# Loading one block of A in two lots, into idle result buffers, in the opening of a tuned matmul

## The chip, the cores and the metric

One core of one Trainium2 chip. The metric is device time in microseconds (us) of one execution; medians are over several runs. A profile is of one execution; its "span", from first to last instruction, is 1.7 us shorter than the device time of the same execution.

A load is issued by GpSimd; DMA engines then move the data, and the load has landed when the last of its 16 completions has counted up its semaphore (a counter that others can wait for). In the lines shown, PE is TensorE, PEld its weight loads, DVE VectorE, ACT ScalarE, POOL GpSimd; a timeline has start, length, engine, line, what, and in brackets the idle time before it and what ended that.

## The reference

```python
def setup_inputs():
    m, k, n = 4096, 4096, 4096
    # a (m, k), b (k, n), bias (n,), all float32, normally distributed
def reference(a, b, bias):
    return np.tanh(np.matmul(a, b) + bias)
```

The kernel casts A and B to 16-bit floats while loading. The product is 8192 TensorE matmuls of 128 x 128 by 128 x 512.

## The kernel before

Only the opening matters. There TensorE must start before A and B are there, so it works on eight row tiles (group 0: tiles 0 to 3, group 1: tiles 4 to 7) and takes the 32 depth tiles of A and B in blocks. All these loads but those of B's first two depth tiles go through one queue, GpSimd's. A load of A is four issues, one for each quarter of the partitions; VectorE then transposes it, and only then can TensorE use it.

```python
    AN = 3                                   # buffers "an" for loads of A
    anat = ctx.enter_context(tc.tile_pool(name="anat", bufs=AN))
    opool = ctx.enter_context(tc.tile_pool(name="opool", bufs=4))   # results "o_sb"
    ...
    def load_a(m0, nmb, t0, nt):
        an = anat.tile([P, nmb, nt * QP], fp16, name="an")
        for t, n in split(t0, nt):
            for q in (0, 2, 1, 3):
                ...
                nc.gpsimd.dma_start(out=an[ds(q * QP, QP), :, ...], in_=...)
        return an
    ...
    def pump():                              # issue loads in order while a buffer is free
        while queue and (queue[0][0] is None or live[0] < AN):
            ...
    # the order of the loads
    want_a("g1a", 2, 4 * P, 2 * Q, 0, BL)    # group 1, depth tiles 0-3, two row tiles
    want_a("g1a2", 2, 6 * P, 2 * Q, 0, BL)
    want_a("g1b", G, 4 * P, G * Q, BL, BL)   # group 1, depth tiles 4-7
    for i in range(BL):
        want(load_b_next)                    # B, depth tiles 4-7
    want_a("g0b", G, 0, G * Q, BL, BL)       # group 0, depth tiles 4-7   <- the change
    want_a("g0c", G, 0, G * Q, KS, KM - KS)  # group 0, depth tiles 8-15
    for u in range(KS, KM, 2):
        want(lambda u=u: load_b_all(u, 2))   # B, depth tiles 8 and 9 first
    ...
```

The four result buffers hold something else first: the first block of group 0 ("nat"), which TensorE transposes at 6.5 to 9.8 us. Then they lie idle until the main loop.

Of the kernel before, what the change touches and what calls it, by code (L numbers as in the profile page):

```python
# [14 lines left out]
P = 128  # L15
Q = 4
QP = 32
NB = 512
fp32 = mybir.dt.float32
fp16 = mybir.dt.float16  # L20
# [3 lines left out]
def kernel(  # L24
# [18 lines left out]
    G = 4  # L43
    KS = 8
    AN = 3
    BL = 4
# [5 lines left out]
    anat = ctx.enter_context(tc.tile_pool(name="anat", bufs=AN))  # L52
    atp = ctx.enter_context(tc.tile_pool(name="atp", bufs=4))
    biasp = ctx.enter_context(tc.tile_pool(name="biasp", bufs=2))
    opool = ctx.enter_context(tc.tile_pool(name="opool", bufs=4))
# [22 lines left out]
    def split(t0, nt):  # L78

        low = [(t, BL) for t in range(t0, min(t0 + nt, KS), BL)]  # L80
        t = max(t0, KS)
        return low + ([(t, t0 + nt - t)] if t0 + nt > t else [])

    def load_a(m0, nmb, t0, nt):
        an = anat.tile([P, nmb, nt * QP], fp16, name="an")
        for t, n in split(t0, nt):
            for q in (0, 2, 1, 3):
                k = t * P + q * BL * QP if t < KS else P * KS + (q * (KT - KS) + t - KS) * QP
                src = a[ds(m0, nmb * QP), ds(k, n * QP)]
                nc.gpsimd.dma_start(  # L90
                    out=an[ds(q * QP, QP), :, ds((t - t0) * QP, n * QP)],
                    in_=src.rearrange("(mb p) k -> p mb k", p=QP),
                )
        return an

    def transpose_a(at, an, mb0, t0, nt):

        for t, n in split(t0, nt):
            order = "P mb (k t) -> P mb t k" if t < KS else "P mb (t k) -> P mb t k"
            nc.vector.transpose(  # L100
                at[:, ds(t, n), :].rearrange("P t (mb p) -> P mb t p", p=QP),
                an[:, ds(mb0, Q), ds((t - t0) * QP, n * QP)].rearrange(order, k=QP),
            )
# [9 lines left out]
    queue, live, staged = [], [0], {}  # L113

    def pump():
        while queue and (queue[0][0] is None or live[0] < AN):
            key, uses, load = queue.pop(0)
            made = load()
            if key is not None:
                live[0] += 1  # L120
                staged[key] = [made, uses]

    def want_a(key, uses, *where):
        queue.append((key, uses, lambda: load_a(*where)))

    def want(load):
        queue.append((None, 0, load))

    def turn(at, key, mb0, t0, nt):
        pump()  # L130
        transpose_a(at, staged[key][0], mb0, t0, nt)
        staged[key][1] -= 1
        if not staged[key][1]:
            live[0] -= 1
            pump()

    def mm(ps, at, bt, t, j, start, stop):
# [4 lines left out]
    def finish(ps, addend, mi, c0, w=NB, o_sb=None, queues=(nc.sync,)):  # L142
# [22 lines left out]
    ats = [  # L165
        bpool.tile([P, KT, P], fp16, name=f"atx_{m}", tag=f"b_{4 + m}") for m in range(G)
    ] + [atp.tile([P, KT, P], fp16, name="at") for m in range(G)]
# [41 lines left out]
    def down(ps, ms, t0, t1, done):  # L209
        for m in ms:  # L210
            for j in range(J):
                for t in range(t0, t1):
                    mm(ps[m][j], ats[m], b_cur, t, j, False, t == t1 - 1)
                done(ps[m][j], m, j)
# [73 lines left out]


    want_a("g1a", 2, 4 * P, 2 * Q, 0, BL)  # L290
    want_a("g1a2", 2, 6 * P, 2 * Q, 0, BL)
    want_a("g1b", G, 4 * P, G * Q, BL, BL)
    for i in range(BL):
        want(load_b_next)
    want_a("g0b", G, 0, G * Q, BL, BL)
    want_a("g0c", G, 0, G * Q, KS, KM - KS)
    for u in range(KS, KM, 2):
        want(lambda u=u: load_b_all(u, 2))
# [3 lines left out]
    for t in (KM, KM + 8):  # L302
        want_a(("g1", t), G, 4 * P, G * Q, t, 8)
        want(lambda t=t: load_b_all(t, TB))
        if t > KM:
            want(lambda: load_bias(bias_bc, 0, nc.gpsimd))
        want(lambda t=t: load_b_all(t + TB, TB))
    for m in g0:
        want_a(("g0", m), 1, m * P, Q, KM, KT - KM)
    todo = [(c, mi) for c in range(NC) for mi in range(MT) if (c, mi) >= (0, 2 * G)]  # L310
    pump()


    for i in range(G):
        turn(ats[G + i], "g1a2" if i > 1 else "g1a", i % 2 * Q, 0, BL)
    down(ps, g0, BL - 1, BL, put_aside)
    for i in range(G):
        turn(ats[G + i], "g1b", i * Q, BL, BL)
# [1 line left out]
    one_by_one(ps, g1, 0, BL, 0)  # L320
    across(ps, g1, BL, KS - 1, 0)
    for m in g0:
        turn(ats[m], "g0b", m * Q, BL, BL)
    down(ps, g1, KS - 1, KS, put_aside)


# [127 lines left out]
```

## Time and profile before

| | before |
|---|---|
| device time, median (six runs) | 1781.6 us (1781.4 to 1782.1) |
| span of the profiled execution | 1780.6 us |
| TensorE busy | 1774.4 us, 100% |
| GpSimd busy (writing loads) | 872.5 us, 49% |
| VectorE busy | 763.7 us, 43% |

A busy TensorE can hide short stalls, since each matmul is recorded with 0.38 us while the next one starts 0.215 us behind it. So the reading goes by the distance between starts. The prediction below shows the lines. Its "chain of waits" is the work that ended last, followed back from the last instruction, each piece to what released it.

### The profile page before, as it was taken

To read this page: it belongs to the slowest core of one execution; us is meant where nothing else is said; L and a number is where in the kernel's file an instruction comes from. 1 tells how busy PE (TensorE), PEld (TensorE's weight loads), DVE (VectorE), ACT (ScalarE), POOL (GpSimd) and SP (SyncE) were. 2 spreads that over 40 slices of the span, in tenths; PEclk is the share of its full clock that TensorE was granted. 3 is DMA by queue.
4 is the path that set the end of the run, shared out by engine and by line. 5 is a ranking of instruction groups with operands and counts; after the bars stand their busy time and mean duration, and the time that the engine had idled before them with its cause. 6 is when DMAs were issued, how large, how long until landed. Compare 5 with 4: busy or idle time off the path is not lost.

```text
span 1780.6 us, 20859 instructions
## 1 busy us (share of the span) xinstructions
PE 1774.4 (100%) x8254; PEld 807.0 (45%) x8254; DVE 763.7 (43%) x682; ACT 172.9 (10%) x281; POOL 872.5 (49%) x1618
## 2 busy tenths in 40 slices
PE   9999999999999999999999999999999999999999
PEld 4444444444444444444444444444444444444444
DVE  3574443444334443444344443444344443444342
ACT  2021000000000000000000000000000000000001
POOL 7465566544565554444456554444544445444510
PEclk9999999999999999999999999999999999999999
DMA  9999999976999877767699997766777667766731
GB/s 183 205 193 177 173 162 166 141 125 110 166 176 164 145 112 116 118 116 120 113 168 173 159 149 116 119 115 109 129 116 121 107 108 121 119 114 109 117 77 42
DMA packets 281393, 238.94 MB, mean 134 GB/s; under 512 B 159056, under 2 KB 231760, under 8 KB 281296
## 3 DMA queue, kind: packets, MB, share of 16 engines
q0 software_dynamic: 243280, 167.88, 69.9%
q1 hardware_dynamic: 37728, 69.62, 11.0%
q8 instruction: 64, 1.05, 0.3%
q14 instruction: 33, 0.27, 0.0%
q10 hardware_dynamic: 288, 0.13, 0.0%
HBM read 337.64 MB, written 67.11 MB: 227 GB/s over the span
## 4 chain that ended last, share of the span: by engine, by line
PE 98%; DMA 1%; POOL 0%; issue 0%; DVE 0%; ACT 0%; POOLq 0%; DVEq 0%
PE ps L415 93%; PE ps L138 5%; DMA an<-in_a_dram 1%; DMA b<-in_b_dram 0%; POOL an L90 0%; POOL nat L246 0%; ACT o_sb L152 0%; DVE atx L100 0%; DVE o_sb L149 0%; POOL b L69 0%; POOL ident L264 0%; POOLq L264 0%; DVEq L149 0%; DVEq L100 0%; POOLq L438 0%
## 5 line engine op out<-in xcount | busy, mean ns | idle before, releaser
L415 PE MATMUL ps<-b,at 128*128 128x512 f16 x7712 | 1657.8, 378 | 0.0
L90 POOL DMA_DIRECT2D an<-in_a_dram x1492 | 805.9, 547 | 797.1 <-DVE at L100 558.6
L415 PEld LDWEIGHTS <-at 128*128 128x128 f16 x7712 | 754.6, 98 | 903.3
L100 DVE STREAM_TRANSPOSE at<-an 128x512 f16<-128x512 f16 (+1 forms) x380 | 565.5, 1539 | 78.2 <-DMA an<-in_a_dram 78.2
L149 DVE TENSOR_TENSOR o_sb<-ps,bias_bc 128x512 f32<-128x512 f32 (+1 forms) x243 | 165.6, 683 | 907.3 <-PE ps L415 697.7
L152 ACT ACTIVATE o_sb<-o_sb 128x512 f32<-128x512 f32 (+1 forms) x243 | 151.4, 624 | 1501.2 <-DVE o_sb L149 1501.2
L73 POOL DMA_DIRECT2D b<-in_b_dram x104 | 56.2, 544 | 14.1 <-DMA an<-in_a_dram 7.0
L138 PE MATMUL ps<-b,atx 128*128 128x512 f16 x256 | 56.2, 379 | 0.6 <-DVE atx L100 0.6
L138 PE MATMUL ps<-b,at 128*128 128x512 f16 x256 | 55.6, 379 | 0.0
L138 PEld LDWEIGHTS <-at 128*128 128x128 f16 x256 | 25.0, 98 | 30.2
L138 PEld LDWEIGHTS <-atx 128*128 128x128 f16 x256 | 24.8, 98 | 30.6 <-DVE atx L100 1.6
L100 DVE STREAM_TRANSPOSE atx<-an 128x512 f16<-128x512 f16 (+2 forms) x12 | 16.3, 1399 | 11.7 <-DMA an<-in_a_dram 11.7
L69 POOL DMA_DIRECT2D b<-in_b_dram x12 | 7.8, 654 | 22.4 <-PE ps L415 22.3
L152 ACT ACTIVATE spill<-spill 128x512 f32<-128x512 f32 x16 | 9.9, 630 | 84.4 <-DVE spill L149 84.4
L149 DVE TENSOR_TENSOR spill<-ps,spill 128x512 f32<-128x512 f32 x16 | 10.2, 674 | 6.2 <-PE ps L138 6.2
L181 DVE TENSOR_TENSOR spill<-spill,bias_bc 128x512 f32<-128x512 f32 x16 | 10.3, 681 | 3.5 <-DMA bias_bc<-in_bias_dram 3.5
L173 ACT COPY spill<-ps 128x512 f32<-128x512 f32 x16 | 8.0, 624 | 12.8 <-PE ps L138 12.8
L228 PE MATMUL ps<-zeros 128*128 128x512 f16 (+1 forms) x14 | 4.7, 504 | 1.3 <-DVE zeros L221 1.3
L176 DVE TENSOR_TENSOR spill<-ps,spill 128x512 f32<-128x512 f32 x8 | 4.8, 674 | 0.0
L228 PEld LDWEIGHTS <-zeros 128*128 128x128 f16 x14 | 1.6, 130 | 3.7 <-issue 2.5
L246 POOL DMA_DIRECT2D nat<-in_a_dram x4 | 2.3, 587 | 0.8 <-POOLq L438 0.8
L239 DVE CAST b<-spill 128x1024 f16<-128x1024 f32 x1 | 0.7, 694 | 4.3 <-DMA spill<-in_b_dram 4.3
(14 smaller groups left out, 9.1 us busy)
## 6 DMA issues: line engine op xcount, KB each, us to landing
an<-in_a_dram POOLq DMA_DIRECT2D x480, 192.0 KB, 5.1
out_dram<-o_sb SPq DMA_DIRECT2D x239, 256.0 KB, 2.7
an<-in_a_dram POOLq DMA_DIRECT2D x960, 32.0 KB, 2.7
b<-in_b_dram POOLq DMA_DIRECT2D x94, 256.0 KB, 8.1
b<-in_b_dram POOLq DMA_DIRECT2D x6, 1024.0 KB, 12.5
an<-in_a_dram POOLq DMA_DIRECT2D x32, 128.0 KB, 5.3
out_dram<-spill SPq DMA_DIRECT2D x16, 256.0 KB, 5.1
an<-in_a_dram POOLq DMA_DIRECT2D x12, 256.0 KB, 8.3
```

The source lines that it names most:

```text
L69: queue.dma_start(out=dst, in_=src[:, ds(t0 % BL, nt), :])
L73: nc.gpsimd.dma_start(out=bt[t0 // TB][ds(q * QP, QP), ds(t0 % TB, nt), :], in_=src.rearrange("(t p) n -> p t n", p=QP),)
L90: nc.gpsimd.dma_start(out=an[ds(q * QP, QP), :, ds((t - t0) * QP, n * QP)], in_=src.rearrange("(mb p) k -> p mb k", p=QP),)
L100: nc.vector.transpose(at[:, ds(t, n), :].rearrange("P t (mb p) -> P mb t p", p=QP), an[:, ds(mb0, Q), ds((t - t0) * QP, n * QP)].rearrange ...
L138: nc.tensor.matmul(ps, at[:, t, :], bt[t // TB][:, t % TB, ts(j, NB)], start=start, stop=stop)
L149: nc.vector.tensor_tensor(out=o_sb[:, piece], in0=ps[:, piece], in1=addend[:, piece], op=mybir.AluOpType.add)
L152: nc.scalar.activation(o_sb[:, piece], o_sb[:, piece], mybir.ActivationFunctionType.Tanh)
L173: nc.scalar.copy(aside(m, j), ps)
L176: nc.vector.tensor_tensor(out=aside(m, j), in0=ps, in1=aside(m, j), op=mybir.AluOpType.add)
L181: nc.vector.tensor_tensor(out=aside(m, j), in0=aside(m, j), in1=bias_bc[:, ts(j, NB)], op=mybir.AluOpType.add)
L228: nc.tensor.matmul(ps[:, ds(0, w)], zeros[:, :P], zeros[:, :w], start=i == 0, stop=i == n - 1)
L415: nc.tensor.matmul(ps, at[:, t, :], b_cur[t // TB][:, t % TB, ds(c0, w)], start=t == 0, stop=t == KT - 1,)
```

## The change

(`turn` transposes a row tile out of a landed load; `live[0]` counts the "an" buffers in use.) Its intent: g0b is the load on which TensorE waits in the opening. Cut in two lots, the first half should come sooner. Loads of one block for two row tiles (g1a, g1a2 and the lots) are as large as a result buffer, so they go there and leave the three "an" buffers to others.

```diff
     def load_a(m0, nmb, t0, nt):
-        an = anat.tile([P, nmb, nt * QP], fp16, name="an")
+        small = nmb * nt * QP == 2 * NB
+        pool, tag = (opool, "o_sb") if small else (anat, "an")
+        an = pool.tile([P, nmb, nt * QP], fp16, name="an", tag=tag)
 ...
     def pump():
-        while queue and (queue[0][0] is None or live[0] < AN):
+        while queue and live[0] + queue[0][3] <= AN:     # small loads hold no "an"
 ...
-    want_a("g0b", G, 0, G * Q, BL, BL)
+    want_a("g0b", 2, 0, 2 * Q, BL, BL)
+    want_a("g0b2", 2, 2 * P, 2 * Q, BL, BL)
 ...
-        turn(ats[m], "g0b", m * Q, BL, BL)
+        turn(ats[m], "g0b2" if m > 1 else "g0b", m % 2 * Q, BL, BL)
```

More of the change, by code (lines that the diff above doesn't have):

```diff
@@ L115, in pump @@
     def pump():
-        while queue and (queue[0][0] is None or live[0] < AN):
-            key, uses, load = queue.pop(0)
+        while queue and live[0] + queue[0][3] <= AN:
+            key, uses, load, held = queue.pop(0)
             made = load()
+            live[0] += held
             if key is not None:
-                live[0] += 1
-                staged[key] = [made, uses]
+                staged[key] = [made, uses, held]
     def want_a(key, uses, *where):
-        queue.append((key, uses, lambda: load_a(*where)))
+        held = int(where[1] * where[3] * QP != 2 * NB)
+        queue.append((key, uses, lambda: load_a(*where), held))
     def want(load):
-        queue.append((None, 0, load))
+        queue.append((None, 0, load, 0))
     def turn(at, key, mb0, t0, nt):
@@ L133, in turn @@
         if not staged[key][1]:
-            live[0] -= 1
+            live[0] -= staged[key][2]
             pump()
```

## The prediction

> **What bounds the kernel now.** I first read the busy shares and the chain of waits on the page. TensorE is at 100% and the granted clock is 9 (90% or more) in every slice, so nothing in steady state is waiting for a load. The chain of waits in order of time says where TensorE is not yet alone:
>
> ```profile
> 4.48 6.52 DMA b<-in_b_dram
> 11.00 0.28 issue
> 11.29 2.48 POOL an L90 x4
> 13.76 5.41 DMA an<-in_a_dram
> 19.18 0.28 issue
> 19.46 9.00 DMA an<-in_a_dram
> 28.46 0.03 DVEq L100
> 28.49 0.05 issue
> 28.54 0.72 DVE atx L100
> 29.26 0.05 issue
> 29.31 7.08 PE ps L138 x32
> 36.39 0.06 issue
> 36.44 83.04 PE ps L138 x384
> 119.48 1654.20 PE ps L415 x7680
> ```
>
> Columns: start, length, what. The last piece gives the rate: 1654.20 us / 7680 = 215.4 ns per matmul. From 29.31 on there remain 32 + 384 + 7680 = 8096 matmuls; 8096 x 0.2154 = 1743.9, and the chain has 7.08 + 0.06 + 83.04 + 1654.20 = 1744.38. So after 29.31 TensorE loses under 0.5 us in all. Loads can only be worth what is lost before that, and two places are left. The TensorE timeline from 28 to 36.5 us:
>
> ```profile
> 27.94 0.81 PE L138 MATMUL ps<-b,at 128*128 128x512 f16 x3
> 29.31 7.51 PE L138 MATMUL ps<-b,atx 128*128 128x512 f16 x33 [0.56 <-DVE atx L100]
> ```
>
> **Gap 1** is group 0's second block: the last matmul of group 1 starts at 28.37, the next at 29.31, a distance of 0.94 us where 0.215 is normal: **0.72 us lost**. It waits for the first transposition, which waits for "g0b" (the load of 16 row quarters that the change cuts in two); its fourth issue left at 19.46 and landed at 28.46. **Gap 2**: 32 matmuls from 29.31 should end at 36.20; the 33rd starts at 36.44: **0.23 us lost**. Section 4 gives it to "issue"; the weight-load view blames VectorE. The wait instructions of TensorE in the trace say otherwise: one on two DMA semaphores runs from 35.10 to 36.38, and the semaphore that ended it is that of the fourth quarter of B's tiles 8 and 9. The transposition needed there ended at 35.17. The DMA view of that issue alone (28.74 us) gives its landing as 28.74 + 7.6 = 36.35:
>
> ```profile
> b<-in_b_dram POOLq DMA_DIRECT2D x1, 128.0 KB, 7.6
> ```
>
> So right behind the wait that the change attacks stands a second one, for B, on the same GpSimd queue.
>
> Next I asked what holds these loads up: their buffers, or the queue. The GpSimd timeline from 16 us:
>
> ```profile
> 16.54 1.99 POOL L90 DMA_DIRECT2D an<-in_a_dram x3
> 19.46 0.65 POOL L90 DMA_DIRECT2D an<-in_a_dram x1 [0.93 <-DMA an<-in_a_dram]
> 21.20 0.65 POOL L90 DMA_DIRECT2D an<-in_a_dram x1 [1.09 <-DVE at L100]
> 22.16 0.65 POOL L90 DMA_DIRECT2D an<-in_a_dram x1 [0.32 <-DMA b<-in_b_dram]
> 25.13 0.65 POOL L90 DMA_DIRECT2D an<-in_a_dram x1 [2.32 <-DMA b<-in_b_dram]
> 26.03 0.65 POOL L90 DMA_DIRECT2D an<-in_a_dram x1 [0.26 <-DMA b<-in_b_dram]
> 26.67 1.11 POOL L73 DMA_DIRECT2D b<-in_b_dram x2
> ```
>
> The loads of this queue use eight completion semaphores in turn, so issue n waits until issue n-8 has landed: landings at 19.18, 21.88, 24.84 and 25.75 are followed by issues at 19.46, 22.16, 25.13 and 26.03, 0.28 us later each. **At most eight loads are in flight, whatever their size.** The buffers don't hold: g0b takes the buffer of g1a, whose last read ended at 13.9, yet g0b is issued only at 16.54, straight behind the loads ahead of it. The 21.20 issue is put down to VectorE, but its semaphore turn (landing 20.64) also ended just before.
>
> The stretches 19.2 to 28.5 and 28.5 to 36.4 show the DMA engines at 1.40 and 1.23 of a full share and 187 and 196 GB/s: the queue always has work. What arrives when is set by the bytes ahead in the queue.
>
> **What the Trainium skill says.** "TensorE: Matmul & The Clock Gate", section "Wait — 56ns, not 53.3ns?": 215.7 ns between matmuls of 512 columns at full clock; the trace has 215.4, so steady state has nothing to give. "DMA: Bandwidth & Descriptors", section "Anatomy of one DMA — SWDGE (gpsimd) path": a fixed cost of about 2 us per GpSimd load, and DMA engines do not wait on semaphores, the issuing sequencer does. The trace agrees on the second (the 0.28 us pairs above); for the first, an issue at 11.29 landed 2.7 us later with little ahead of it. Same page, "Latency and other measured facts": some of the 16 DMA engines are usually slower. In the trace, 15 of the 16 completions of the B load that ends gap 2 are there at 35.02, the last at 36.35; the lag is 1.3 us for every load from 25.75 to 38.9, so one engine is behind. No page speaks of the eight in flight.
>
> **The change part by part.**
> (1) g1a and g1a2 go into result buffers. These held the four first blocks ("nat"), which TensorE transposes at 6.51, 7.17, 8.28 and 9.37, so g1a's first issue can't leave at 5.00 any more but at about 7.0 (6.92 is the end of the first four transpositions). At 0.6 us each: 7.0, 7.6, 8.2, 8.8, then g1a2 9.4, 10.0, 10.6, and its fourth needs the landing of 11.00, so 11.29 as before. The queue works on B until 11.00, so g1a still lands at 11.4 to 12.5. Cost 0 to 0.15 us on everything behind.
> (2) g0b in two lots of four issues of 64 KB instead of four of 128 KB. Lot 1 is issued at 16.5, 17.1, 17.8, 19.46. The four landed at 26.22 to 28.46, 0.75 us apart; half the bytes are 0.37 apart, so lot 1 ends at 25.75 + 4 x 0.37 = 27.2. The first transposition (0.72) ends at 28.0, before TensorE needs it (28.59): **gap 1 closes, -0.72 us**. Lot 2 lands by about 28.7; row tile 2 needs it at 32.
> (3) Four more issues, some 4 x 0.6 = 2.4 us of GpSimd, and four more turns of the eight semaphores. Lot 2 takes the turns of g0c: 20.92, 22.16, 25.13, 26.03. g0c is issued at 26.7, 27.3, 28.0, 28.6, where before it left from 21.20 on. Its first part lands (estimate) 27.3 + about 1.6 (what 2.7 leaves without 0.6 of issue and 0.4 of data) + 1.33 = 30.2 instead of 29.77, the queue running dry for a moment; its fourth near 34.2 instead of 33.80. B's tiles 8 and 9 follow 2.55 us later: 36.8 instead of 36.35.
> (4) The hold count no longer lets g1a, g1a2, g0b use up the three "an" buffers. By the finding above no buffer held, so 0. Rotation in both pools shifts by whole rounds (four more result buffers of four, three fewer of three): the main loop is unchanged.
>
> **Sum.** TensorE reaches tile 8 at 35.5 instead of 36.2, and waits there until B lands plus 0.09: 36.44 before, about 36.9 now. The 0.72 us of gap 1 comes back as a longer gap 2, plus 0.45 for the later issue: +0.1 to +0.6 with the lagging engine as it was.
>
> **The rivals.**
> A. B for tiles 8 and 9 lands no later, or earlier, since the lag of one engine is an accident of the run: with all 16 completions where the other 15 are, B lands at 35.1, g0c at 32.5, and both gaps go: -0.9 us. For: the lag vanishes by itself at 41 us. Against: lag was there in the profiled run[...].
> B. Transpositions of g0c become the wait: four of 1.15 us from 34.3 on end at 35.5, 36.6, 37.8, 38.9, needed at 36.9, 37.8, 38.6, 39.5. Close, but behind B; if g0c is 0.5 later still, another +0.3.
> C. The wait of GpSimd for the first transpositions starves the queue and g1b is late: it has 1.7 us of slack (first transposition done 19.9, needed 21.66), B's tile 6 0.27 (24.84, needed 25.1). A delay of 0.5 costs 0.2 there and is absorbed by gap 2.
> D. The author's hope, gap 1 closed and kept: -0.7. Against it stands gap 2.
>
> **Range and chances.** I give the carry-over (+0.1 to +0.6) most weight, A and D together about a quarter, B and C little: 1781.73 + 0.3 = 1782.0. The runs before spread over 0.6 us. Low 1780.9 is A with noise; high 1783.1 is B and a dry queue of 1 us. Two per cent is 35.6 us; all idle TensorE time in the opening is about 1 us behind 9.6 us, so anything but the same would need a broken steady state.
>
> **What would show it.** Right: no gap before group 0's second block; one of 0.8 to 1.5 us before tile 8, released by B; g1a issued near 7.0; g0c issued near 26.7 and landing near 34.2; from there 215.4 ns. Wrong: tile 8 starts before 36.2 (A or D), or a new gap between 21 and 27 us (C), or loads waiting in the main loop.

## The result, and the profile after

| | before | after |
|---|---|---|
| device time, median (six runs each) | 1781.6 us (1781.4 to 1782.1) | 1783.37 us (1782.99 to 1783.81) |
| span of the profiled execution | 1780.6 us | 1781.5 us |

The ratio is 1.001 (95% interval 0.9997 to 1.0022). Ratios here are the mean time of one kernel's runs over that of the other's in the same rounds, so not quite the ratio of the medians. The interval includes 1, so the times alone settle little. But the six runs of each kernel do not overlap, and the medians differ by 1.77 us, which has a cause, as the profiles and experiments show. The time lies 0.27 us above the predicted range.

The chain of waits of the kernel after, in order of time (start, length, what):

```profile
25.14 3.12 POOL an L93 x5
28.27 1.57 POOL b L73 x3
29.83 7.22 DMA b<-in_b_dram
37.06 0.14 issue
37.19 83.15 PE ps L142 x384
120.35 1654.20 PE ps L420 x7680
```

The chain no longer goes through g0b. It goes through GpSimd, eight issues without a break and the ninth behind them, which is the load of B that ends the wait. TensorE's timeline of the same execution, from 28 us:

```profile
28.62 7.07 PE L142 MATMUL ps<-b,atx 128*128 128x512 f16 x32
37.19 0.59 PE L142 MATMUL ps<-b,atx 128*128 128x512 f16 x2 [1.51 <-DMA b<-in_b_dram]
```

Group 0's second block starts at 28.62 without a gap, 0.69 us earlier than before. But depth tile 8 starts at 37.19 instead of 36.44. The matmul ahead of it starts at 35.31, so 1.887 - 0.215 = 1.67 us are lost there. GpSimd's timeline of the same execution says why:

```profile
7.26 7.16 POOL L93 DMA_DIRECT2D an<-in_a_dram  x12 [2.23 <-PE ps L232]
...
17.14 1.76 POOL L93 DMA_DIRECT2D an<-in_a_dram  x3 [0.56 <-DMA an<-in_a_dram]
19.40 0.58 POOL L93 DMA_DIRECT2D an<-in_a_dram  x1 [0.50 <-DMA an<-in_a_dram]
21.70 0.58 POOL L93 DMA_DIRECT2D an<-in_a_dram  x1 [1.73 <-DMA b<-in_b_dram]
22.63 0.58 POOL L93 DMA_DIRECT2D an<-in_a_dram  x1 [0.35 <-DMA b<-in_b_dram]
23.89 0.58 POOL L93 DMA_DIRECT2D an<-in_a_dram  x1 [0.68 <-DMA b<-in_b_dram]
25.14 3.12 POOL L93 DMA_DIRECT2D an<-in_a_dram  x5 [0.68 <-DMA b<-in_b_dram]
```

17.14 to 19.40 are lot 1. 21.70, 22.63, 23.89 and the first of the five at 25.14 are lot 2: each waits for the landing of a B load eight issues earlier. Only then, at 25.71, does g0c leave; before, it had these very places and left at 21.20. At 25.71 only small loads are in flight, and they have all landed at 27.90. The first part of g0c lands at 30.48 (the DMA view of the issues at 25.7: count, size, us to landing):

```profile
an<-in_a_dram POOLq DMA_DIRECT2D x1, 256.0 KB, 4.8
```

That is 2.58 us later, although its 256 KB take 1.33. In the stretch 26.5 to 29.5 us the DMA engines moved less (the last number of the line, GB/s; the one ahead of it is their busy share). Before:

```profile
26.50:29.50 3.00, 2.44 (x12) 0.92 (x11) 0.96 (x2) 2.23 (x5) 2.31 (x5) 1.00 1.46 195
```

After:

```profile
26.50:29.50 3.00, 3.00 (x16) 1.35 (x15) 2.55 (x4) 2.19 (x5) 3.00 (x6) 1.00 1.10 123
```

(195 - 123) GB/s x 3 us = 0.216 MB less, which at 195 GB/s is 1.1 us of the queue's time. The queue ran dry. It did so for longer than this stretch: from 25 to 30 us, microsecond by microsecond, the DMA engines moved 143, 87, 75, 150 and 186 GB/s after the change and 182, 193, 196, 195 and 196 before. That is 0.32 MB less, or 1.6 us: the 0.89 us by which B's tile 7 had landed sooner than in the profile before (24.86, not 25.75) and the 0.71 us by which B's tiles 8 and 9 landed later.

### The profile page after: what moved, and what is told of

Its sections match the earlier page's. It is cut to its first block, busy times and chain, and to the rows that moved or that the text cites. A ratio compares the mean times of both kernels' runs of the same rounds, so it can differ in the third digit from the quotient of the medians.

```text
span 1781.5 us, 20870 instructions
## 1 busy us (share of the span) xinstructions
PE 1774.8 (100%) x8254; PEld 807.1 (45%) x8254; DVE 763.9 (43%) x682; ACT 173.0 (10%) x281; POOL 874.0 (49%) x1622
## 3 DMA queue, kind: packets, MB, share of 16 engines
q8 instruction: 64, 1.05, 0.2%
## 4 chain that ended last, share of the span: by engine, by line
PE 98%; DMA 1%; POOL 1%; issue 0%; ACT 0%; DVE 0%; DVEq 0%; POOLq 0%
PE ps L420 93%; PE ps L142 5%; DMA b<-in_b_dram 1%; POOL an L93 1%; DMA nat<-in_a_dram 0%; POOL b L69 0%; POOL b L73 0%; ACT o_sb L156 0%; DVE o_sb L153 0%; PE tp L261 0%; PE ps L232 0%; DVEq L153 0%; POOLq L443 0%
## 5 line engine op out<-in xcount | busy, mean ns | idle before, releaser
L142 PEld LDWEIGHTS <-at 128*128 128x128 f16 x256 | 25.1, 98 | 30.3 <-issue 0.2
```

What stands on the lines that cost most here:

```text
L142: nc.tensor.matmul(ps, at[:, t, :], bt[t // TB][:, t % TB, ts(j, NB)], start=start, stop=stop)
```

## The experiments

Theory D: **the queue runs dry**, because at most eight loads are in flight and eight half-size ones hold too few bytes to cover the time until the next one gets going. Rival W: what costs is GpSimd's wait for the result buffers (2.23 us at 7.26). Rival I: what costs is the time of four more issues. Theory L is about the kernel before: its two gaps depend on how far the slowest DMA engine lags in an execution.

One bookkeeping carries all of it. For each profile I added up what TensorE lost behind the last of its opening transpositions: each distance between starts over 0.24 us, less the normal 0.2154. In all fourteen profiles, span less this loss less the start of that last transposition is 1770.10 to 1770.13 us. So nothing else moves the end of these profiled executions, and span is about 1779.7 us plus the loss.

| profile | gap before group 0's second block | gap before tile 8 | all lost | span |
|---|---|---|---|---|
| before, six looks | 0.72, 0.73, 0.09, 0.08, 0.24, 0.69 | 0.22, 0.23, 0.23, 0.22, 0.22, 0.21 | 0.94, 0.96, 1.07, 0.30, 0.46, 1.05 | 1780.6, 1780.8, 1780.8, 1780.0, 1780.1, 1780.7 |
| after, three looks | none | 1.67, 1.74, 2.65 | 1.79, 1.74, 2.65 | 1781.5, 1781.4, 1782.3 |
| result buffers only | none | 0.16 | 0.33 | 1780.2 |
| split only | none | 2.35 | 4.04 | 1783.7 |
| woven order | none | 0.07 | 0.07 | 1779.8 |
| tiny loads | 0.23 | 2.81 | 3.04 | 1782.8 |
| four lots | none | 5.33 | 7.22 | 1787.0 |

("None" is a normal distance. What the gaps leave of a loss are short stalls from 49 us on, and in two kernels matmuls at half clock, told below.)

### Both kernels again, and the two parts apart

These four ran on one chip, each with five timed runs; the kernel before had a median of 1781.91 us (1781.51 to 1782.96).

The kernel before, once more:

```diff
 (no edit)
```

> The kernel before, unchanged, measured against itself. Question: are the two gaps that its first profile showed (0.72 us before group 0's second block, 0.23 us before tile 8 of B) its normal state? Theory L (one lagging DMA engine was an accident of the profiled execution): this trace has neither gap, span about 1779.8 us, 15th and 16th completion of the loads around 24 us within 0.4 us. Rival: the gaps are there in every execution, span 1780.6 us. Time: ratio 1.000 in both.

Measured: 1782.73 us (1782.14 to 1783.08), ratio 1.0004. The same program differs from itself by 0.8 us in the median, so that is the floor of noise between two loads of a program. The profile showed both gaps again, and the 16th completion 0.6 us behind the 15th. Theory L was not supported by this look.

The changed kernel, once more:

```diff
 (no edit of the changed kernel)
```

> The changed kernel, unchanged. Theory D (the queue runs dry, because eight half-size loads fill the eight places in flight): no gap before group 0's second block, a gap of 1.4 to 1.9 us before tile 8, and between the landing of lot 2 and that of the next load (first part of g0c) 2.3 to 2.7 us where its bytes take 1.33. Time +1.5 to +2.0 us over before. Rival L2 (an accident of one execution): gap below 1 us, time +0.5.

Measured: 1783.53 us, one run at 1785.7, ratio 1.0012 (0.9999 to 1.0026). Gap before tile 8 1.74 us; lot 2 landed at 27.64 and the first part of g0c at 29.97, 2.33 us later. As theory D expected. The run at 1785.7 had a granted clock of 0.999.

The first part of the change alone:

```diff
 (the changed kernel, with)
-    want_a("g0b", 2, 0, 2 * Q, BL, BL)
-    want_a("g0b2", 2, 2 * P, 2 * Q, BL, BL)
+    want_a("g0b", G, 0, G * Q, BL, BL)
-        turn(ats[m], "g0b2" if m > 1 else "g0b", m % 2 * Q, BL, BL)
+        turn(ats[m], "g0b", m * Q, BL, BL)
```

> g1a and g1a2 in the result buffers, g0b in one lot as before. Theory D: nothing runs dry, g1a is issued at 7.2 instead of 5.0 us but lands at the same 11.4, time within 0.3 us of before. Rival W (GpSimd's wait for the result buffers is what costs): +1.5 to +2.0 us as in the changed kernel.

Measured: 1781.82 us, ratio 1.0002. TensorE's timeline:

```profile
27.76 1.24 PE L142 MATMUL ps<-b,at 128*128 128x512 f16 x5
28.84 8.52 PE L142 MATMUL ps<-b,atx 128*128 128x512 f16 x38
```

No gap is marked at group 0's second block, and the stream runs on past tile 8. g0c left at 21.26 us and its first part landed at 29.20, 1.30 behind g0b: the queue was full. Rival W falls: the wait for the result buffers is there and costs nothing.

The second part alone, the split in the old buffers:

```diff
 (the kernel before, with)
-    want_a("g0b", G, 0, G * Q, BL, BL)
+    want_a("g0b", 2, 0, 2 * Q, BL, BL)
+    want_a("g0b2", 2, 2 * P, 2 * Q, BL, BL)
-        turn(ats[m], "g0b", m * Q, BL, BL)
+        turn(ats[m], "g0b2" if m > 1 else "g0b", m % 2 * Q, BL, BL)
```

> g0b in two lots, but in the buffers of before; g1a leaves at 5.0 us again. Theory D: the whole loss, +1.5 to +2.0 us, with the same late issue of g0c (near 25.7 us) and the same gap before tile 8. Rival W: within 0.3 us of before.

Measured: 1783.8 us (1783.06 to 1786.01), ratio 1.0014 (1.0001 to 1.0026). g0c left at 26.25, its first part landed 2.87 us behind the last of lot 2. The whole loss is in the split. The gap before tile 8 was 2.35 us, not the "same" as I expected, and the profiled run took 1785.43 us and shows something more. Two stretches (busy time and count of TensorE, its weight loads, VectorE, ScalarE, GpSimd; then the granted clock, DMA share, GB/s):

```profile
30.00:38.00 8.00, 5.82 (x28) 2.48 (x26) 2.78 (x3) 1.27 (x3) 4.69 (x10) 1.00 1.29 200
38.00:42.00 4.00, 4.00 (x12) 1.46 (x11) 1.84 (x2) 0.00 (x0) 3.22 (x6) 0.58 1.11 191
```

Just behind the gap of 2.35 us the granted clock is 0.58: seven distances between starts are 0.427 us, twice the normal one, and two lie between; by the bookkeeping this costs 4.04 - 2.35 = 1.7 us. So a gap can cost more than its own length. The four lots below showed it too; gaps of 2.65 and 2.81 us in other profiles did not. The clock record tells them apart. In all fourteen profiles each stretch of full clock, and both stretches of half clock inside a kernel, lasted a whole multiple of 3.41 us; here the clock was half from 38.62 to 42.03. The 3.41 us ahead of the half clock held 2.35 us of gap here and 2.33 us with the four lots. The gaps of 2.65 and 2.81 us fell across the end of such a step, and no step held more than 1.82 and 1.85 us of them. In these profiles, then, it mattered how much of a gap fell into one step, not only how long it was; where the limit lies between 1.85 and 2.33 us is not shown.

The unprofiled runs fit: the granted clock was 0.999 in one of five timed runs of the changed kernel (1785.7 us), two of the split alone (1785.43 and 1786.01) and one of the tiny loads below (1785.71), 0.998 in all five of the four lots, and full in every run of the kernel before, the result buffers alone and the woven order.

### Order, number and size of the loads

These four ran on another chip, five timed runs each; the kernel before had 1782.06 us (1781.58 to 1783.21).

The same issues in another order, with parts of g0c woven between the lots:

```diff
 (the changed kernel, with two more arguments of load_a, the quarters and the buffer, and)
     want_a("g0b", 2, 0, 2 * Q, BL, BL)
+    want_a("g0c", G, 0, G * Q, KS, KM - KS, (0, 2))      # two of its four parts
     want_a("g0b2", 2, 2 * P, 2 * Q, BL, BL)
-    want_a("g0c", G, 0, G * Q, KS, KM - KS)
+    want(lambda: load_a(0, G * Q, KS, KM - KS, (1, 3), staged["g0c"][0]))
```

> The whole change with another order of the same issues: lot 1, first two parts of g0c, lot 2, last two parts of g0c. Same buffers, bytes and number of issues. Theory D (the queue runs dry because eight small loads fill the eight places): with two 256 KB parts in the eight, no dry spell: each load lands its own bytes' time after the one before, tile 8 of B lands at 35.1 to 35.9 instead of 37.06, gap before tile 8 0 to 0.4 us, time within 0.6 us of before. Rival I (four more issues on GpSimd are what costs) and rival W (result buffers): +1.5 to +2.0 us, as the issues are as many.

Measured: 1782.21 us, ratio 1.0000 (0.9987 to 1.0012). Its chain of waits, from the first matmuls on:

```profile
9.83 108.84 PE ps L143 x504
118.68 1654.20 PE ps L422 x7680
```

One piece of 504 matmuls: the chain leaves TensorE nowhere behind 9.83 us. The stretch 26.5 to 29.5 us:

```profile
26.50:29.50 3.00, 3.00 (x15) 1.37 (x14) 0.95 (x2) 2.15 (x5) 2.36 (x5) 1.00 1.58 180
```

180 GB/s instead of 123. Same buffers, same number of issues, same bytes: rivals W and I fall together, and D stands. It is the best profile of all (0.07 us lost), yet its time is that of the kernel before, within noise. No version here beats the kernel before.

The kernel before, with four tiny loads that only take places:

```diff
     want_a("g0b", G, 0, G * Q, BL, BL)
+    tiny = singles.tile([P, 4, 16], fp16, name="tiny")
+    for i in range(4):        # 4 KB each, result unused
+        want(lambda i=i: nc.gpsimd.dma_start(out=tiny[:, i, :], in_=a[ds(0, P), ds(i * 16, 16)]))
     want_a("g0c", G, 0, G * Q, KS, KM - KS)
```

> The kernel before with four tiny loads (4 KB each, result unused) between g0b and g0c; g0b in one lot. Theory D: the tiny ones take the four places that g0c had, g0c leaves near 26.5 instead of 21.2 us, its first part lands 0.5 to 1 us later than in the kernel before and the gap before tile 8 is 0.6 to 1.4 us; time +0.4 to +1.2 us. Rival S (the halving of g0b itself, its packets or its transpositions, is what costs): 0 to +0.2 us.

Measured: 1784.55 us, ratio 1.0014 (1.0001 to 1.0026). GpSimd's timeline:

```profile
20.76 0.56 POOL L299 DMA_DIRECT2D tiny<-in_a_dram  x1 [0.73 <-DMA b<-in_b_dram]
21.99 0.55 POOL L299 DMA_DIRECT2D tiny<-in_a_dram  x1 [0.67 <-DMA b<-in_b_dram]
24.57 0.53 POOL L299 DMA_DIRECT2D tiny<-in_a_dram  x1 [2.03 <-DMA b<-in_b_dram]
25.54 0.53 POOL L299 DMA_DIRECT2D tiny<-in_a_dram  x1 [0.43 <-DMA b<-in_b_dram]
26.50 2.59 POOL L90 DMA_DIRECT2D an<-in_a_dram  x4 [0.43 <-issue]
```

16 KB in all, and g0c leaves at 26.50 instead of 21.2 us. The direction is as theory D has it, and rival S falls, since g0b is whole here. The size was missed: the loss before tile 8 is 2.81 us, twice what I expected at most, and the time rose by 2.5 us where I expected 0.4 to 1.2. The later issue (26.50, 25.71 in the changed kernel) is not why: the first part of g0c landed at 30.38, 0.1 us sooner than there, and as late against the kernel before as expected. But the third part landed 2.75 us behind the second, where its bytes take 1.33, and these 1.4 us are the excess. Such an extra lag came in three of the six dry profiles (0.5, 0.6 and 1.4 us); its cause stays open.

The change carried on, g0b in four lots of 32 KB issues:

```diff
 (the changed kernel, with a pool "lots" of four buffers, and)
-    want_a("g0b", 2, 0, 2 * Q, BL, BL)
-    want_a("g0b2", 2, 2 * P, 2 * Q, BL, BL)
+    for m in g0:
+        want_a(("g0b", m), 1, m * P, Q, BL, BL)
-        turn(ats[m], "g0b2" if m > 1 else "g0b", m % 2 * Q, BL, BL)
+        turn(ats[m], ("g0b", m), 0, BL, BL)
```

> The change carried on: g0b in four lots of one row tile, sixteen issues of 32 KB. Theory D: only about 1.5 us of data in flight, GpSimd's 0.57 us per issue and the 2 us to landing decide; g0c leaves near 30.3 us, tile 8 of B lands near 40, gap before tile 8 about 4.5 us, time +4.5 to +7 us (the upper end if TensorE runs at half clock for a while after the gap, as in the run of the split alone). Rival L2 (the loss is an accident of DMA engines and does not grow with the number of issues): +1.5 to +2.5 us.

Measured: 1789.64 us, ratio 1.0041 (1.0029 to 1.0054). TensorE's timeline at tile 8:

```profile
40.98 0.58 PE L145 MATMUL ps<-b,atx 128*128 128x512 f16 x1 [5.17 <-DMA b<-in_b_dram]
```

g0c left at 29.92 us (30.3 expected), B's tiles 8 and 9 landed at 40.85 (40 expected). 5.33 us are lost in the gap (about 4.5 expected) and 1.9 behind it at half clock. The time is 7.6 us over the kernel before, above the 4.5 to 7 expected. The loss grows with the number of small issues; rival L2 falls.

The kernel before a third time:

```diff
 (no edit)
```

> The kernel before once more, as the floor of noise between two loads of one program and a third look at its two gaps. Theory L (how far one DMA engine lags differs from execution to execution): the gaps add up to anything from 0 to 1 us, and span and lag go together. Time within 0.9 us of before.

Measured: 1782.04 us, ratio 0.9999. The gap before group 0's second block was 0.09 us, where the second look had 0.73, but short stalls from 49 us on made up for it, 1.07 us in all. What those later stalls are was not followed up.

### More looks at the kernel before

Three looks at the kernel before and one at the changed kernel, without timed rounds, on one chip.

```diff
 (no edit in any of the four)
```

> The kernel before, one profiled look. So far every profiled run obeys span = 1779.7 us + the time TensorE loses behind its first matmuls, and device time = span + 1.7 us. Theory L: the loss of the kernel before varies from execution to execution between 0 and 1 us with the lag of the slowest DMA engine, so a run near 1781.5 us shows gaps of 0.1 to 0.3 us in all and its loads around 24 to 36 us end with a 16th completion less than 0.5 us behind the 15th or all of them earlier. Rival: the gaps always add up to 0.95 us and the faster unprofiled runs have another cause.

> As the first look: span minus 1779.7 us equals the sum of the gaps within 0.15 us, whatever it is; theory L expects it to differ from that of the other looks, the rival 0.95 us again.

> A third look at the kernel before: the sum of its gaps again equals span minus 1779.7 us; theory L expects another sum, the rival 0.95 us.

> The changed kernel, one more look. Theory D: gap before tile 8 of 1.5 to 2.0 us and 2.3 to 2.7 us between the landings of lot 2 and of the first part of g0c, whatever the lag of the slowest engine; span 1779.7 us plus the gaps.

Measured: 1781.69, 1781.81 and 1782.4 us for the kernel before, with 0.30, 0.46 and 1.05 us lost; 1784.08 for the changed kernel with 2.65 us lost and 2.72 us between lot 2 and the first part of g0c. The 2.65 us missed the 1.5 to 2.0 expected; the second part of g0c landed 1.90 us behind the first, one of the extra lags told above. TensorE's timeline in the first look:

```profile
27.74 1.03 PE L138 MATMUL ps<-b,at 128*128 128x512 f16 x4
28.68 8.59 PE L138 MATMUL ps<-b,atx 128*128 128x512 f16 x38
```

and in the third:

```profile
27.69 1.03 PE L138 MATMUL ps<-b,at 128*128 128x512 f16 x4
29.25 7.94 PE L138 MATMUL ps<-b,atx 128*128 128x512 f16 x35 [0.53 <-DVE atx L100]
```

The same program waits for g0b in one execution and hardly in another. The rival (always 0.95) falls, and so does the first half of theory L's reading: it is the landing of g0b's last part, anywhere from 27.83 to 28.61 us, that differs, but the lag of one engine alone does not order the looks (the 16th completion of g0b's last part was 0.46 us behind the 15th in the first look, 0.42 in the third). All that is shown is that arrival varies by 0.8 us and the loss with it.

## Why the prediction was wrong

The path was right: gap 1 closes, and the wait for B before tile 8 takes its place. Two terms of the sum had the wrong size: the time from the end of an issue to its landing when the queue has run dry (1.6 us put, 2.8 in the changed kernel's profile), and the loss of the kernel before (0.95 us put, 0.2 in the median run).

- **Gap 1 closes:** right. Lot 1 had landed at 26.36 us (27.2 predicted), and no profile with the split has this gap.
- **It comes back before tile 8, released by B:** right. In all six looks at before, tile 8 starts 0.09 us behind the landing of B, and B's part lands 7.9 us behind g0b's last part. The two loads stand at a fixed distance in one queue, so the second wait is whatever the first one leaves.
- **The wait for the result buffers, 0 to 0.15 us:** right. g1a left at 7.26 and landed from 11.39 us (11.43 before); with the result buffers alone the time is that of before.
- **The turns of the eight semaphores delay g0c:** right in kind, shown by the tiny loads and the woven order. It left at 25.71 us, 1 us before the 26.7 predicted, since B's tile 7 had landed at 24.86 and not at 25.75.
- **"The queue running dry for a moment", B at 36.8 instead of 36.35:** this term of the sum failed in size. I put 1.6 us between the end of an issue and the landing, without the bytes' own time. I took it from the load issued at 11.29 "with little ahead of it", and that reading was wrong: seven loads issued before it had yet to land, the last at 13.67, so its 2.7 us measured a full queue. Measured where the queue ran dry, 30.48 - 26.36 (end of the issue) - 1.33 = 2.8 us; over six dry profiles 1.9 to 2.9 (three looks at the changed kernel, split alone, tiny loads, four lots). How much of it is one load's own delay is not shown, since the loads ahead were still landing 0.8 to 1.7 us after the issue's end. With that, an issue ending at 27.3 would have given 31.4 and B near 38. As g0c left a us earlier, B landed at 37.06: that 36.8 came so close is luck, two errors that partly cancelled. Tile 8 starts 0.75 us later than before, not 0.45; another 0.12 is a short stall at 50.8 us.
- **1781.73 as the time of an execution that loses 0.95 us:** this was wrong too, and weighs as much. The profiled execution took 1782.33 us, 0.6 more than the 1781.73 (the median of the three runs that I had). By the bookkeeping, 1781.6 - 1.7 - 1779.7 = 0.2 us is what the median execution of before lost, about what gap 2 alone took in all six looks, while the median of the changed kernel lost 1783.37 - 1.7 - 1779.7 = 2.0. I had 0.95 and 1.4 for the two. The change closed a gap that the median run, by this sum, did not have. (The sum varies with the session: the medians of before on the two other chips, 1781.91 and 1782.06 us, give 0.5 and 0.7.)
- **Rivals:** A, the late landing is an accident, is half true of the kernel before, where gap 1 came and went (0.08 to 0.73 us in six looks) and gap 2 stayed at 0.21 to 0.23; but the dry spell of the changed kernel comes in every look. B and C were not seen. D, the gain kept, was seen in the woven order alone, and there only in the profile: against the median run there is next to nothing left to gain (0.2 us by the sum above).

## What to carry to other kernels

Ask how many loads a queue lets be in flight, and count bytes, not loads: cutting a load in two halves what those places cover, and the price is paid by the next large load, which leaves later. If a load must be cut, weave the halves with large ones. And before a gap of under a microsecond is hunted, compare the profiled execution's time with the median: a gap that the median run does not have can't be won. Where a gap may reach 2 us, look at the granted clock behind it too.

## What the Trainium skill lacked or had wrong

- No page says how many loads of one queue are in flight. In this program it was eight, set by eight completion semaphores in turn: four loads of 4 KB put the next large load back from 21.2 to 26.50 us and cost 2.5 us.
- "DMA: Bandwidth & Descriptors", section "Anatomy of one DMA — SWDGE (gpsimd) path", has a fixed cost of about 2 us per load. In six dry profiles the landing came 1.9 to 2.9 us behind the end of the issue instruction, over and above the 1.33 us of the bytes; with the issue's own 0.65 us, 2.5 to 3.6. It is no clean measure of one load, as the loads ahead were still landing for 0.8 to 1.7 us of it. The same page's section "Rules for kernel authors" advises to coalesce many small transfers into a large one. The four lots bear it out (7.6 us over the kernel before), but the woven order has small loads too and cost nothing measurable (1782.21 us, 1782.06 before): what counted was how many of the eight places small loads held at once.
- "TensorE: Matmul & The Clock Gate", section "What's actually happening", ties the half clock to at least one idle window of about 3.4 us. Here 2.35 us without a matmul in one step of 3.41 us were enough: the next step ran at half clock, with matmuls 0.427 us apart. 1.85 us in one step were not enough.
